# Two steps of a hybrid SSD and pooling trunk's first layer moved to later places in each engine's queue

## The chip, the cores and the metric

The kernel runs on one core of a Trainium2 chip. A core has five engines with a queue each: TensorE (PE, matrix products), VectorE (DVE), ScalarE (ACT), GpSimd (POOL) and SyncE (SP, which here only issues DMAs). An engine works through its queue in order, and an instruction at the head that waits for another engine holds up all behind it. The metric is the device time of one execution in microseconds; lower is better.

## The reference, cut to what matters

The kernel computes one inference step of two layers for 1024 prompt tokens and 64 sample tokens (8 sequences of 8), 1088 columns in all, with 1024 model channels:

```
hn   = rmsnorm(x, g) * (1 + scale) + shift        # scale, shift from the conditioning
z, xbc, dt = split(hn @ w_in)                     # first layer, 2048 + 4096 + 32 columns
xbc  = silu(causal_conv4(xbc))                    # 4 taps along the tokens
y    = ssd_scan(xbc, softplus(dt))                # chunked state space recurrence
x    = x + (1 + gate) * (norm(y * silu(z)) @ w_out)
hn   = ...; pooling layer with u, z = hn @ w_in   # second layer
y    = rmsnorm(x + ...)
```

All of it is float32. A product of two float32 numbers is made on TensorE from three products of parts: each operand is split into `hi`, its leading part, and `lo`, the difference.

## The kernel before, in words

Channels lie on the 128 partitions and tokens along the free dimension, so `x` is eight tiles of 128x1088, the channel tiles k = 0 to 7. The change touches the first layer's front only, the first 360 us or so of the program.

**Scaling.** `front` (L1308) goes over the eight channel tiles. For each, an `ada` product on TensorE gives the scale and shift (L253, L262; DVE reads them in L271 and L272), and `modulate` (L311) makes the scaled tile (DVE L316), its `hi` part (`hh`, ACT L322), its `lo` part (`hl`, DVE L323, which needs `hh`), the tile itself with its shift (ACT L324) and the same for the sample columns (L329 to L333). TensorE then multiplies tile k with two weight tiles (L182 to L184: `hi` by `hi`, `lo` by `hi`, `hi` by `lo`, in three column chunks each) and with the dt weights (`pdt`, L1354). After the eighth tile two more weight tiles follow in the same form, whose evictions to `z` are `gate_chunk`s on ACT (L869).

**Activation differences.** The other columns of the first layer are multiplied by a scheme with seven half-size products for two weight tiles at once (`fast_pair`, L992) in place of eight. It needs differences of blocks of the activations: `act_sums_front` (L1375) makes sixteen half tiles by DVE subtractions (`sub`, L1382, in place on `x`) and splits the results into `hi` (ACT L1385) and `lo` (DVE L1386): four tiles each for the products T2, T3 and T4, and for T1 into the upper half of `hn`. Its steps are traced behind the six `gate_chunk`s of the two weight tiles after the scaling, under `issue_after(the gate chunk)`, and in the first pair.

**Pairs.** `front_pairs` (L1416) makes twelve pairs in the order of the list FRONT: z2, z3, z4, b5, x5, z5, b7, x7, z6, b0, x0, z7. Each pair is the seven products B11, B21, T2, T3, T1, T4, B22, of 24 matmuls of 272 columns each (L987 to L989; L989 is the one that needs the weight's `lo`). The weights of a pair are sums and differences of four blocks made on POOL (L952 to L959, `sw` and `wr`), each split by `split_half` (L168): `hi` on ACT (L174) and `lo` on DVE, the fourth and sixth of a pair on POOL (L176). Every product call first has the split of three products later traced. So the POOL splits of a pair serve T3 and T4, and the one traced in B21 serves T1. Products are added up by DVE from PSUM (`put` and `add`, L998), and B11 is copied by ACT (L1013).

**Convolution.** A b or x pair ends with `proj_end` for both its tiles: `conv_tile` (L336) makes the first tap on ACT (L351), three taps on DVE for the 1024 prompt columns and the 64 sample columns (L349), and the silu on ACT (L352); the result goes to DRAM (L1448). In the kernel before, this is traced behind B22 of the same pair.

**dt.** `dt_phase` (L438) turns `pdt` into step sizes in a chain of small DVE and ACT operations (L443 to L506), with exponentials on ACT (L452, L479, L483) between silu evaluations, and copies on POOL (L436).

**What sets the order.** The instructions are written in plain order; when the program is built, a scheduler lays them into each engine's queue by the order in which they were traced and its own estimate of when they can start. `issue_after(i)` adds one constraint: instructions that the block traces on the engine of `i` stand behind `i`. A `gate_chunk` is an ACT instruction, so in the kernel before it holds back the ACT part of the activation differences and not their DVE part.

Of the kernel before, what the change touches and what calls it, by code (L numbers as in the profile page):

```python
# [2 lines left out]

# [4 lines left out]
F32 = mybir.dt.float32  # L8
F32R = mybir.dt.float32r
AF = mybir.ActivationFunctionType  # L10
ALU = mybir.AluOpType
# [86 lines left out]
class Build:  # L98
# [212 lines left out]
    def modulate(self, l, k, x, rst, hi, lo, a, n, t):  # L311

        nc = self.nc
        pn = min(a + n, NP) - a
        sh = self.shf[l][:, k, 8:9]
        nc.vector.scalar_tensor_tensor(out=t[:, :pn], in0=x[:, a:a + pn], scalar=self.scl[l][:, k, 8:9], in1=rst[:, a:a + pn], op0=ALU.mult, op1=ALU.mult)  # L316
        if l:
            nc.scalar.activation(t[:, :pn], t[:, :pn], AF.Identity, bias=sh)
            nc.scalar.activation(hi[:, a:a + pn], t[:, :pn], AF.Copy)
            nc.vector.tensor_tensor(out=lo[:, a:a + pn], in0=t[:, :pn], in1=hi[:, a:a + pn].bitcast(F32), op=ALU.subtract)  # L320
        else:
            nc.scalar.activation(hi[:, a:a + pn], t[:, :pn], AF.Identity, bias=sh)  # L322
            nc.vector.scalar_tensor_tensor(out=lo[:, a:a + pn], in0=t[:, :pn], scalar=sh, in1=hi[:, a:a + pn].bitcast(F32), op0=ALU.add, op1=ALU.subtract)  # L323
            nc.scalar.activation(t[:, :pn], t[:, :pn], AF.Identity, bias=sh)  # L324
        if pn < n:
            s = slice(NP, TOK)
            ts = t[:, pn:n].rearrange("p (b i) -> p b i", i=8)
            eng = nc.gpsimd if l and k % 2 == 0 else nc.vector
            eng.tensor_tensor(out=t[:, pn:n], in0=x[:, s], in1=rst[:, s], op=ALU.mult)  # L329
            eng.tensor_tensor(out=ts, in0=ts, in1=self.scl[l][:, k, 0:8].unsqueeze(2).to_broadcast([P, 8, 8]), op=ALU.mult)  # L330
            eng.tensor_tensor(out=ts, in0=ts, in1=self.shf[l][:, k, 0:8].unsqueeze(2).to_broadcast([P, 8, 8]), op=ALU.add)
            nc.scalar.activation(hi[:, s], t[:, pn:n], AF.Copy)
            eng.tensor_tensor(out=lo[:, s], in0=t[:, pn:n], in1=hi[:, s].bitcast(F32), op=ALU.subtract)  # L333


    def conv_tile(self, ti, raw, dst, ncv, scan):  # L336
# [172 lines left out]
    def scan_group(self, g, T):  # L509
# [167 lines left out]

        load_ac(0)
        F = [front(0)]
        yield  # L680
        F.append(front(1))
        yield
        for c in range(0, 8, 2):
# [624 lines left out]
    def front(self):  # L1308

        nc, io, sl = self.nc, self.io, self.slots  # L1310
        xs = self.xs
        wdts = sl.get("wdt")
        wdt = wdts[:, :256].rearrange("p (k m) -> p k m", k=8)
        nc.sync.dma_start(wdt, io["wdt"])
        rst = sl.get("rst")
        with self.ln_set():
            nc.scalar.activation(rst, xs[0], AF.Square)
            for k in range(1, 8):
                sq = self.raw_tile()
                for a, n in CH if k == 7 else ((0, TOK),):  # L1320
                    nc.scalar.activation(sq[:, a:a + n], xs[k][:, a:a + n], AF.Square)
                    nc.vector.tensor_tensor(out=rst[:, a:a + n], in0=rst[:, a:a + n], in1=sq[:, a:a + n], op=ALU.add)
            for a, n in CH:
                self.ms_log(rst, rst, a, n, 1.0 / 1024, "mm", 3)
                self.rstd(rst[:, a:a + n])
        self.ada_first(0)
        self.hn = []

        self.wslots = []
        for i in range(2):  # L1330
            self.stream_split(i, True)
        self.ada_first(1)
        ws = [self.wsplit.pop(i) for i in range(2)]
        self.wpos = 2
        pst = [[self.mm_tile() for _ in range(3)],
               [self.pp.tile([P, 512], F32, tag=t, bufs=b, name=self.name("p0")) for t, b in (("y", 2), ("y", 2), ("S", 1))]]
        pdt = self.pp.tile([P, 512], F32, tag="tr", bufs=2, name="pdt")
        for k in range(8):
            if k < 6:
                self.ada_first(k + 2)  # L1340
            if k == 4:
                self.stream_split(2)
            if k == 6:
                self.stream_split(3)
            hi, lo = sl.get("hh", F32R), sl.get("hl", F32R)
            for a, n in CH if k == 0 else ((0, TOK),):
                self.modulate(0, k, xs[k], rst, hi, lo, a, n, xs[k][:, a:a + n])
            self.hn.append((hi, lo))
            for i in range(2):
                for c in range(3):  # L1350
                    self.mm1(pst[i][c], ws[i], k, (hi, lo), CH[c], k == 0, k == 7)
            for j in range(4):
                n = 320 if j == 3 else 256
                nc.tensor.matmul(pdt[32 * j:32 * j + 32, :n], wdt[:, k, :], xs[k][:, 256 * j:256 * j + n],  # L1354
                                 start=k == 0, stop=k == 7, tile_position=(0, 32 * j))
        sl.free(rst, wdts, *self.wslots)
        dt = self.dt_phase(pdt)
        next(dt)
        for i in range(2):
            dst = sl.get("z")  # L1360
            for c in range(3):
                self.gate_chunk(dst, c, pst[i][c])
            self.gate_store(i, dst)
        ops = self.act_sums_front()
        for i in range(2):
            w, dst = self.stream_next(), sl.get("z")
            for c, ch in enumerate(CH):
                ps = self.mm_tile()
                self.mm3(ps, w, self.hn, ch)
                with self.tc.issue_after(self.gate_chunk(dst, c, ps).ins):  # L1370
                    next(ops)
            self.gate_store(2 + i, dst)
        self.front_pairs(ops, dt)
# [42 lines left out]
    def front_pairs(self, ops, dt):  # L1416

        nc, sl = self.nc, self.slots
        self.fast_init(len(FRONT))
        self.G, G = {}, None  # L1420
        for n, (kind, g) in enumerate(FRONT):
            if kind == "z":
                ts = [sl.get("z") for _ in range(2)]
                outs = [(t, 0, None) for t in ts]
            else:
                if kind == "b":
                    self.G[g] = G = self.proj_open(g)
                ii = 2 * (kind == "x")
                ts = [self.proj_begin(G, ii + i) for i in range(2)]
                outs = [(t, 3, t[:, 1027:1115].rearrange("p (b w) -> p b w", w=11)[:, :, 3:11]) for t in ts]  # L1430

            def after(x):
                if kind == "z" and x in ("z01", "z11"):
                    a = HALF * int(x[1])
                    self.z_chunk(ts[1], ts[1][:, a:a + HALF], a, HALF)
                elif kind == "z" and x in ("B21", "B22"):
                    a = HALF * (x == "B22")
                    self.z_chunk(ts[0], ts[0][:, a:a + HALF], a, HALF)
                    if x == "B22":
                        self.gate_store(2 * g, ts[0])  # L1440
                elif kind == "z" and x == "T4":
                    self.gate_store(2 * g + 1, ts[1])
                if kind != "z" and x == "B22":
                    for i in range(2):
                        self.proj_end(G, ii + i, ts[i])
                        if g:
                            t = G["out"].pop()
                            nc.sync.dma_start(self.xbd[g][ii + i], t)  # L1448
                            sl.free(t)
                if n == 0 and x in ("B11", "B21"):  # L1450
                    next(ops)
                if n < 2 and x in ("B21", "T3", "T4"):
                    next(dt, None)
                if n == len(FRONT) - 1:
                    if x in ("T2", "T3"):
                        sl.free(*[self.T[int(x[1]), k] for k in range(4)])
                    elif x == "T1":
                        for k in range(4):
                            for i in range(2):
                                nc.sync.dma_start(self.hn[k][i][:, HALF:].bitcast(F32), self.b12d[2 * k + i])  # L1460

            self.fast_pair(*outs, after)
        sl.free(*[self.T[4, k] for k in range(4)])

    def ssd_layer(self):
# [351 lines left out]
```

## Time and profile before

| what | value |
|---|---|
| median of 3 runs | 1618.24 us (1616.37 to 1619.92) |
| profiled execution: time | 1620.23 us |
| profiled execution: span, first to last instruction | 1618.5 us |
| TensorE busy over the span | 1581.7 us (98%) |
| DVE, ACT, POOL busy | 1288.2, 796.5, 500.8 us |
| mean granted TensorE clock | 0.993 |

A row of the timeline gives the start and the length of an instruction (or of several alike, x2), its engine, source line, operation, output and inputs, and in brackets how long the engine had been idle before it and what ended that. A row of the waits names the waiting engine and tile and who was waited for, then the sum, the count and the longest, in us. A row of windows gives a stretch, its length, the busy time of TensorE, of its weight loads, of DVE, ACT and POOL, then the granted TensorE clock, the DMA share and GB/s. The busy time of TensorE is not its time at peak, since its matmuls overlap; its idle times are what can be won.

### The profile page before, as it was taken

The numbers are of one execution on the slowest core, as the hardware profiler recorded it, in microseconds if no ns is written. First come the engines' busy times: TensorE is split into PE (matmuls) and PEld (weight loads), VectorE is DVE, ScalarE is ACT, GpSimd is POOL, SyncE is SP. The second block draws the span as 40 slices with busy tenths as digits, with TensorE's granted clock in tenths as the row PEclk, the third lists the DMA queues.
The fourth block names the chain that finished last, engine by engine and source line by source line (L and its number), as shares of the span: only waits on it lengthen the run. The fifth ranks groups of instructions, "written<-read, shape, count | busy, mean of one in ns | idle before, by whom it ended". The sixth has DMA issues, their size and how long they took to land. (4 is left out here: it accounts for less than half of the span.)

```text
span 1618.5 us, 30648 instructions
## 1 busy us (share of the span) xinstructions
PE 1581.7 (98%) x11916; PEld 1506.4 (93%) x11916; DVE 1288.2 (80%) x2148; ACT 796.5 (49%) x1517; POOL 500.8 (31%) x562
## 2 busy tenths in 40 slices
PE   8999999999999999999999999999999999999997
PEld 6799999998889889888898899999999999999997
DVE  5875779778888888788888867988889867577886
ACT  6653344357676766674555436623223233333364
POOL 0133556421221212120212222365666640000241
PEclk8999999999999999999999999999999999999999
DMA  9422232354555454668898632133333379555683
GB/s 344 169 85 91 94 117 69 110 186 139 201 161 175 157 192 148 234 210 300 293 338 279 216 128 93 45 139 115 106 106 103 115 223 364 164 165 180 160 176 120
DMA packets 122305, 275.58 MB, mean 170 GB/s; under 512 B 18192, under 2 KB 59312, under 8 KB 122160
## 3 DMA queue, kind: packets, MB, share of 16 engines
q1 hardware_dynamic: 118128, 260.90, 46.6%
q0 software_dynamic: 4032, 12.72, 4.5%
q8 instruction: 94, 1.54, 0.4%
q14 instruction: 51, 0.42, 0.1%
HBM read 201.12 MB, written 70.23 MB: 168 GB/s over the span
## 5 line engine op out<-in xcount | busy, mean ns | idle before, releaser
L989 PE MATMUL st<-hh,w 128*128 128x272 f32 x832 | 240.7, 289 | 2.1 <-DVE w L176 2.1
L987 PE MATMUL st<-hh,w 128*128 128x272 f32 x832 | 240.1, 289 | 0.0
L988 PE MATMUL st<-hl,w 128*128 128x272 f32 x832 | 239.9, 288 | 0.0
L987 PE MATMUL st<-t,w 128*128 128x272 f32 x624 | 179.7, 288 | 0.0
L989 PE MATMUL st<-t,w 128*128 128x272 f32 x624 | 179.5, 288 | 0.0
L182 PE MATMUL mm<-hh,wh 128*128 128x368 f32 (+1 forms) x528 | 178.7, 338 | 0.7 <-ACT raw L421 0.7
L988 PE MATMUL st<-t,w 128*128 128x272 f32 x624 | 179.2, 287 | 0.0
L183 PE MATMUL mm<-hl,wh 128*128 128x368 f32 (+1 forms) x528 | 173.6, 329 | 0.0
L184 PE MATMUL mm<-hh,wl 128*128 128x368 f32 (+1 forms) x528 | 173.4, 328 | 0.0
L989 PEld LDWEIGHTS st<-hh,w 128*128 128x128 f32 x832 | 156.4, 188 | 3.2 <-DVE w L176 3.2
L174 ACT ACTIVATE w<-wr 128x512 fp32r<-128x512 f32 x104 | 65.7, 631 | 188.8 <-PE st L989 155.5
L988 PEld LDWEIGHTS st<-hl,w 128*128 128x128 f32 x832 | 156.7, 188 | 0.0
L987 PEld LDWEIGHTS st<-hh,w 128*128 128x128 f32 x832 | 156.7, 188 | 0.0
L183 PE MATMUL mm<-gl,wh 128*128 128x368 f32 (+1 forms) x384 | 127.3, 331 | 3.6 <-DVE gl L750 3.5
L182 PE MATMUL mm<-gh,wh 128*128 128x368 f32 (+1 forms) x384 | 130.1, 340 | 0.6 <-ACT raw L419 0.5
L1204 PE MATMUL op<-b,w 128*128 128x272 f32 x448 | 128.9, 288 | 0.7 <-DVE b L1133 0.7
L1203 PE MATMUL op<-b,w 128*128 128x272 f32 x448 | 129.5, 289 | 0.0
L1205 PE MATMUL op<-b,w 128*128 128x272 f32 x448 | 128.9, 288 | 0.0
L184 PE MATMUL mm<-gh,wl 128*128 128x368 f32 (+1 forms) x384 | 127.0, 331 | 0.0
L604 POOL TENSOR_TENSOR hd<-h,cd 128x256 f32<-128x256 f32 x56 | 46.8, 836 | 233.2 <-DVE h L605 118.3
L987 PEld LDWEIGHTS st<-t,w 128*128 128x128 f32 x624 | 117.7, 189 | 0.1
L989 PEld LDWEIGHTS st<-t,w 128*128 128x128 f32 x624 | 117.3, 188 | 0.0
(298 smaller groups left out, 4544.6 us busy)
## 6 DMA issues: line engine op xcount, KB each, us to landing
wr<-win SPq DMA_DIRECT2D x48, 512.0 KB, 4.3
acb<-acd SPq DMA_DIRECT2D x64, 256.0 KB, 4.0
wr<-pin SPq DMA_DIRECT2D x32, 512.0 KB, 3.6
wr<-pout SPq DMA_DIRECT2D x28, 512.0 KB, 3.7
x<-x1d SPq DMA_DIRECT2D x24, 544.0 KB, 6.1
x1d<-x SPq DMA_DIRECT2D x22, 544.0 KB, 3.9
wr<-pout POOLq DMA_DIRECT2D x20, 512.0 KB, 5.7
x<-xT SPq DMA_DIRECT2D x16, 544.0 KB, 6.9
```

The source lines that it names most:

```text
L174: self.nc.scalar.activation(hi, src, AF.Copy)
L182: nc.tensor.matmul(ps[:, :n], hi[:, k, :], ah[:, a:a + n], start=first, stop=False)
L183: nc.tensor.matmul(ps[:, :n], hi[:, k, :], al[:, a:a + n], start=False, stop=False)
L184: nc.tensor.matmul(ps[:, :n], lo[:, k, :], ah[:, a:a + n], start=False, stop=last)
L604: nc.gpsimd.tensor_tensor(out=hd, in0=h[-1], in1=cd.unsqueeze(2).to_broadcast([P, 4, 64]), op=ALU.mult)
L987: nc.tensor.matmul(ps[c][:, :QUART], hi[:, k], xh[:, t], start=(k == 0), stop=False)
L988: nc.tensor.matmul(ps[c][:, :QUART], hi[:, k], xl[:, t], start=False, stop=False)
L989: nc.tensor.matmul(ps[c][:, :QUART], lo[:, k], xh[:, t], start=False, stop=(k == 3))
L1203: nc.tensor.matmul(ps[:, :QUART], hi[:, k], xh, start=k == 0, stop=False)
L1204: nc.tensor.matmul(ps[:, :QUART], hi[:, k], xl, start=False, stop=False)
L1205: nc.tensor.matmul(ps[:, :QUART], lo[:, k], xh, start=False, stop=k == 7)
```

## The change

Two places in the tracing order change; no arithmetic, shape, buffer or engine does.

1. `modulate` returns its last DVE instruction, and the activation differences traced behind the gate chunks stand under a second `issue_after`, that of the eighth channel tile's last DVE instruction. So the DVE subtractions may not stand ahead of it in the DVE queue.
2. The two `proj_end`s of a b or x pair, with the store to DRAM, are kept back as a closure and traced when the next pair has traced its second product, B21.

```
-            nc.vector.tensor_tensor(out=lo[:, a:a + pn], in0=t[:, :pn], in1=hi[:, a:a + pn].bitcast(F32), op=ALU.subtract)
+            last = nc.vector.tensor_tensor(out=lo[:, a:a + pn], in0=t[:, :pn], in1=hi[:, a:a + pn].bitcast(F32), op=ALU.subtract)
...
-            eng.tensor_tensor(out=lo[:, s], in0=t[:, pn:n], in1=hi[:, s].bitcast(F32), op=ALU.subtract)
+            last = eng.tensor_tensor(out=lo[:, s], in0=t[:, pn:n], in1=hi[:, s].bitcast(F32), op=ALU.subtract)
+        return last
...
-                self.modulate(0, k, xs[k], rst, hi, lo, a, n, xs[k][:, a:a + n])
+                last = self.modulate(0, k, xs[k], rst, hi, lo, a, n, xs[k][:, a:a + n])
...
-                with self.tc.issue_after(self.gate_chunk(dst, c, ps).ins):
+                with self.tc.issue_after(self.gate_chunk(dst, c, ps).ins), self.tc.issue_after(last.ins):
                     next(ops)
...
-        self.G, G = {}, None
+        self.G, G, ends = {}, None, []
+
+        def end(G, g, ii, ts):
+            for i in range(2):
+                self.proj_end(G, ii + i, ts[i])
+                if g:
+                    t = G["out"].pop()
+                    nc.sync.dma_start(self.xbd[g][ii + i], t)
+                    sl.free(t)
+
...
+                if x == "B21":
+                    while ends:
+                        ends.pop(0)()
                 if kind != "z" and x == "B22":
-                    for i in range(2):
-                        self.proj_end(G, ii + i, ts[i])
-                        if g:
-                            t = G["out"].pop()
-                            nc.sync.dma_start(self.xbd[g][ii + i], t)
-                            sl.free(t)
+                    ends.append(functools.partial(end, G, g, ii, ts))
...
+        for f in ends:
+            f()
```

What this does to the queues is shown at three places. Source lines of the changed file are higher by 1 up to `modulate` and by 2 behind it (L323 is L324 there, L1382 is L1384).

The DVE queue at channel tiles 5 to 7 before; `x_177`, `x_179`, `x_185`, `x_187`, `x_189` are the tiles 0, 1, 4, 5, 6, `hl_707` is the `lo` part of tile 6 and `am_652` the scale and shift of tile 7:

```order
L331 TENSOR_TENSOR x_187<-x_187,shf_267 128x64
L316 SCALAR_TENSOR_TENSOR x_189<-x_189,scl_269,rst_277 128x1024
L330 TENSOR_TENSOR x_189<-x_189,scl_269 128x64
L333 TENSOR_TENSOR hl_668<-x_187,hh_667 128x64
L331 TENSOR_TENSOR x_189<-x_189,shf_267 128x64
L1382 TENSOR_TENSOR x_185<-x_185,x_177 128x544
L1382 TENSOR_TENSOR x_179<-x_187,x_179 128x544
L271 TENSOR_SCALAR shf_267<-am_652,vec 128x9
L272 TENSOR_SCALAR scl_269<-am_652,adab_265,vec 128x9
L140 TENSOR_TENSOR wl_703<-wr_700,wh_702 128x1024
L323 SCALAR_TENSOR_TENSOR hl_707<-x_189,shf_267,hh_706 128x1024
```

Tile 6's `lo` part comes last here, behind two subtractions and tile 7's scale and shift. The DVE queue at the same place in the changed kernel:

```order
L334 TENSOR_TENSOR hl_668<-x_187,hh_667 128x64
L317 SCALAR_TENSOR_TENSOR x_189<-x_189,scl_269,rst_277 128x1024
L331 TENSOR_TENSOR x_189<-x_189,scl_269 128x64
L332 TENSOR_TENSOR x_189<-x_189,shf_267 128x64
L141 TENSOR_TENSOR wl_703<-wr_700,wh_702 128x1024
L324 SCALAR_TENSOR_TENSOR hl_707<-x_189,shf_267,hh_706 128x1024
L272 TENSOR_SCALAR shf_267<-am_652,vec 128x9
L273 TENSOR_SCALAR scl_269<-am_652,adab_265,vec 128x9
```

The two subtractions are gone from between tile 6's scaling and its `lo` part, and that part now stands ahead of tile 7's scale and shift. All sixteen subtractions stand behind the last instruction of tile 7.

The DVE queue at the end of a convolution (that of pair b5), before; `xbc_2054` and `xbc_2067` are the two results, `w_2120` the `lo` part of the weight for T1 of the next pair, x5, and `raw_2080<-st_2123` and `raw_2080<-st_2124` the two sums of that pair's B21:

```order
L349 SCALAR_TENSOR_TENSOR xbc_2054<-raw_1817,vec,xbc_2054 128x1024
L349 SCALAR_TENSOR_TENSOR xbc_2054<-raw_1817,vec,xbc_2054 128x64
L349 SCALAR_TENSOR_TENSOR xbc_2067<-raw_1820,vec,xbc_2067 128x1024
L176 TENSOR_TENSOR w_2120<-sw_1954,w_2120 128x512
L998 TENSOR_TENSOR raw_2080<-st_2123,u_2086 128x272
L998 TENSOR_TENSOR raw_2080<-st_2124,u_2086 128x272
```

Here the split and the sums come behind the whole convolution. The same in the changed kernel, where tiles traced behind the moved step have other numbers (`xbc_2125`, `xbc_2138`; `w_2094`; `raw_2054`):

```order
L177 TENSOR_TENSOR w_2094<-sw_1954,w_2094 128x512
L1000 TENSOR_TENSOR raw_2054<-st_2097,u_2060 128x272
L351 SCALAR_TENSOR_TENSOR xbc_2125<-raw_1817,vec,xbc_2125 128x64
L351 SCALAR_TENSOR_TENSOR xbc_2125<-raw_1817,vec,xbc_2125 128x1024
L1000 TENSOR_TENSOR raw_2054<-st_2098,u_2060 128x272
L351 SCALAR_TENSOR_TENSOR xbc_2125<-raw_1817,vec,xbc_2125 128x64
L351 SCALAR_TENSOR_TENSOR xbc_2138<-raw_1820,vec,xbc_2138 128x1024
```

The split for T1 now stands ahead of the last four instructions of the convolution, and the two sums stand between them. The same happens at all six b and x pairs; from the next sum on the queue is as before.

The POOL queue in the first pair, z2, before; `w_1012` is the split for T3, `w_1109` the one for T4, and the copy from `raw_772` belongs to the dt phase and waits for DVE L480:

```order
L436 COPY raw_1437<-raw_772 128x128
L176 TENSOR_TENSOR w_1012<-wr_892,w_1012 128x512
L959 TENSOR_TENSOR sw_996<-wr_786,sw_996 128x512
L952 TENSOR_TENSOR sw_1185<-wr_1140 128x512
L953 TENSOR_TENSOR sw_1185<-sw_1185,wr_894 128x512
L176 TENSOR_TENSOR w_1109<-wr_892,w_1109 128x512
L957 TENSOR_TENSOR wr_1140<-wr_894,wr_1140 128x512
```

Here the copy is first and the split for T4 next to last. The POOL queue at that place in the changed kernel:

```order
L177 TENSOR_TENSOR w_1012<-wr_892,w_1012 128x512
L961 TENSOR_TENSOR sw_996<-wr_786,sw_996 128x512
L954 TENSOR_TENSOR sw_1185<-wr_1140 128x512
L438 COPY raw_1437<-raw_772 128x128
L955 TENSOR_TENSOR sw_1185<-sw_1185,wr_894 128x512
L959 TENSOR_TENSOR wr_1140<-wr_894,wr_1140 128x512
L177 TENSOR_TENSOR w_1109<-wr_892,w_1109 128x512
```

The copy now stands between two sums of the next pair's weights, and the split for T4 one place later, behind L959 (L957 before).

Smaller moves: ACT makes four `hi` parts for T1 in a row before the last of T3, and the second and third exponential of the dt phase (L479, L483) stand some 12 ACT instructions later and apart, with one more pair of table loads. In the later pairs the POOL split for T4 stands ahead of the next pair's `raw` preparation (L376, L377), and SP issues the load of `scv` ahead of two stores (L1448) and not behind them. Behind pair z7 every queue is in the old order.

More of the change, by code (lines that the diff above doesn't have):

```diff
@@ L1 @@
 import contextlib
+import functools
 import itertools
@@ L319, in modulate @@
             nc.scalar.activation(hi[:, a:a + pn], t[:, :pn], AF.Copy)
[L320 removed]
+            last = nc.vector.tensor_tensor(out=lo[:, a:a + pn], in0=t[:, :pn], in1=hi[:, a:a + pn].bitcast(F32), op=ALU.subtract)
         else:
             nc.scalar.activation(hi[:, a:a + pn], t[:, :pn], AF.Identity, bias=sh)
[L323 removed]
+            last = nc.vector.scalar_tensor_tensor(out=lo[:, a:a + pn], in0=t[:, :pn], scalar=sh, in1=hi[:, a:a + pn].bitcast(F32), op0=ALU.add, op1=ALU.subtract)
             nc.scalar.activation(t[:, :pn], t[:, :pn], AF.Identity, bias=sh)
```

## The prediction

> **What bounds the kernel now.** I read the page first, then the waits of TensorE in the part that the change touches, then its timeline at these waits, then the engine it waits for. From the page:
>
> ```profile
> PE 1581.7 (98%) x11916; PEld 1506.4 (93%) x11916; DVE 1288.2 (80%) x2148; ACT 796.5 (49%) x1517; POOL 500.8 (31%) x562
> ```
>
> TensorE is idle for 36.8 us of the span of 1618.5, and it is the bound. The change removes no matmul, so it can win only idle time of TensorE, and only in the first 360 us, behind which all queues are as before. The waits of TensorE from 0 to 360 us (sum, count, longest):
>
> ```profile
> PE mm L182 <- ACT hh L322: 2.3, 2, 1.9
> PE st L989 <- DVE w L176: 2.1, 5, 0.4
> PE mm L183 <- DVE hl L323: 2.1, 2, 1.8
> ```
>
> The first row is the start of the scaling, ahead of any activation difference, and stays. The second is a weight's `lo` part that comes late, five times 0.42 us. The third holds one wait of 1.8 us for a tile's `lo` part. So 1.8 + 2.1 = 3.9 us is the most that the change can take from the waits, 0.24% of the time.
>
> **The activation differences.** TensorE, ACT and DVE around the 1.8 us (timeline):
>
> ```profile
> 63.60 0.76 PE L182 MATMUL mm<-hh,w 128*128 128x368 f32 x3
> 64.20 0.49 PE L182 MATMUL p<-hh,w 128*128 128x368 f32 x2
> 66.47 0.43 PE L183 MATMUL mm<-hl,w 128*128 128x368 f32 x1 [1.77 <-DVE hl L323]
> ```
>
> ```profile
> 59.96 1.14 ACT L322 ACTIVATE hh<-x,shf 128x1024 fp32r<-128x1024 f32 x1
> ```
>
> ```profile
> 60.21 3.54 DVE L1382 TENSOR_TENSOR x<-x,x 128x544 f32<-128x544 f32 x2
> 63.67 0.21 DVE L271 TENSOR_SCALAR shf<-am,vec 128x9 f32<-128x9 f32 x1
> 64.00 1.21 DVE L140 TENSOR_TENSOR wl<-wr,wh 128x1024 fp32r<-128x1024 f32 x1
> 65.14 1.27 DVE L323 SCALAR_TENSOR_TENSOR hl<-x,shf,hh 128x1024 fp32r<-128x1024 f32 x1
> ```
>
> `hh` of tile 6 is there at 61.10, but DVE first makes two subtractions for 3.54 us, then tile 7's scale and a weight split, and `hl` comes at 66.41. Without the two, `hl` starts at 65.14 - 3.54 = 61.6 and ends near 62.9; the new queue also puts it ahead of tile 7's scale. TensorE asks for it 0.3 us into the tile, at 63.9: about 1 us to spare. Tile 7 follows with the same work and no subtraction in it. So 1.77 us of waiting goes. Nothing takes its place here, as far as the waits show: of the four in the `hh` and `hl` rows this is the only one behind the first two tiles.
>
> The two subtractions were so slow because POOL worked beside them; POOL, and DVE later, with POOL idle:
>
> ```profile
> 60.15 1.29 POOL L953 TENSOR_TENSOR sw<-sw,wr 128x512 f32<-128x512 f32 x1
> 61.40 1.77 POOL L957 TENSOR_TENSOR wr<-wr,wr 128x512 f32<-128x512 f32 x1
> ```
>
> ```profile
> 71.17 1.35 DVE L1382 TENSOR_TENSOR x<-x 128x544 f32<-128x544 f32 x2
> ```
>
> Two cost 1.35 us alone and 3.54 us beside POOL. This stretch is now met by `hl` of tile 6 and the scaling of tile 7. If they are slowed by the same 2.2 us, `hl` ends near 65.1 in place of 62.9, 1.2 us late, and the gain is 0.6. I take 1.77, since the POOL rows end at 63.2 and the scale of tile 7 stands behind `hl`.
>
> The Trainium skill, "GPSIMD Engine Reference", section "8. Key points", says that GpSimd shares its SBUF interfaces with VectorE and contends with DVE instructions that have two SBUF inputs. The rows agree (1.35 against 3.54 us). By that rule `hl` (L323, two SBUF inputs) pays in full and the sum below would be 1.2 us smaller.
>
> **What the moved differences delay.** All sixteen now start when tile 7's last DVE instruction ends, near 66 us, and take 16 x 0.64 = 10 us (0.64 is the step of the row at 71.17), to some 77 us; before, half of them were made between the tiles, and the last row of them stands only a few behind the one at 71.17. The dt chain and the `lo` splits on DVE follow up to 1.5 us later, while TensorE arrives 1.77 us earlier. So their slack shrinks by about 3 us. The points where it can bite are the weight splits of pair z2. TensorE, ACT, DVE and POOL there:
>
> ```profile
> 97.32 0.29 PE L987 MATMUL st<-hh,w 128*128 128x272 f32 x1
> ```
>
> ```profile
> 112.36 0.28 PE L987 MATMUL st<-t,w 128*128 128x272 f32 x1
> ```
>
> ```profile
> 92.99 1.28 ACT L869 ACT_TABLE_LOAD   x1
> 94.29 0.48 ACT L869 ACTIVATE z<-mm 128x368 f32<-128x368 f32 x1
> ...
> 97.52 0.46 ACT L869 ACTIVATE z<-mm 128x352 f32<-128x352 f32 x1 [0.57 <-PE mm L184]
> ...
> 99.50 0.62 ACT L174 ACTIVATE w<-wr 128x512 fp32r<-128x512 f32 x1
> ```
>
> ```profile
> 99.84 0.68 DVE L176 TENSOR_TENSOR w<-sw,w 128x512 fp32r<-128x512 f32 x1
> ```
>
> ```profile
> 100.20 1.48 POOL L176 TENSOR_TENSOR w<-wr,w 128x512 fp32r<-128x512 f32 x1 [6.49 <-ACT w L174]
> 101.65 1.78 POOL L959 TENSOR_TENSOR sw<-wr,sw 128x512 f32<-128x512 f32 x1
> 107.00 1.35 POOL L952 TENSOR_TENSOR sw<-wr 128x512 f32<-128x512 f32 x1 [3.58 <-DMA wr<-win]
> 108.43 1.66 POOL L953 TENSOR_TENSOR sw<-sw,wr 128x512 f32<-128x512 f32 x1
> 110.05 1.74 POOL L176 TENSOR_TENSOR w<-wr,w 128x512 fp32r<-128x512 f32 x1
> 111.75 1.74 POOL L957 TENSOR_TENSOR wr<-wr,wr 128x512 f32<-128x512 f32 x1
> ```
>
> ```profile
> 117.05 1.28 POOL L959 TENSOR_TENSOR sw<-wr,sw 128x512 f32<-128x512 f32 x1 [3.56 <-DVE w L176]
> ```
>
> B11 starts at 97.32 and T4, the sixth product, at 112.36: 3.0 us each, 0.125 per matmul. T2, the third, needs its `lo` with its third matmul, at 103.6; the DVE row ended at 100.5. That is 3.1 us of slack, of which about 3 goes: a wait of 0 to 0.8 us.
>
> T4 needs its POOL split at 112.36 + 0.25 = 112.61, and it was done at 111.79: 0.8 us of slack. In the new queue TensorE is there at 110.84. The POOL chain hangs on the ACT split at 99.50. ACT's evictions follow TensorE: the one at 94.29 had waited for a table load that is now elsewhere, and starts near 92; four `hi` parts and one more stand ahead of the last eviction where two did, 3 x 0.6 us more (the length of such a part by the row at 99.50), so the split comes near 98.2, 1.3 us earlier, not 1.77. POOL then needs, from the row at 100.20 on: the split for T3, L959, 3.6 us for the DMA, L952, now the copy (128x128; a quarter of the 1.28 of a 128x512 row is 0.3, an estimate), L953, L957 and only then the split for T4. With the lengths of these rows that ends at 111.79 - 1.3 + 0.3 + 1.7 = 112.5, 1.6 us late. With 1.28 us each, which the row at 117.05 shows for POOL undisturbed, the six save up to 2 us and TensorE waits for nothing. A wait at T2 is paid once, since it moves T4's need too. DVE has idle time from 104 us in the new queue, since it waits for the sums of T2 and T3, so I stand nearer to the undisturbed end: a loss of 0.5 us, bounds 0 and 1.6.
>
> The two further table loads on ACT, 2 x 1.28 us, fall between 102 and 112 us; the next splits there are needed 5 us later, so they cost nothing unless ACT is that late.
>
> **The convolutions.** DVE at the end of pair b5's convolution, the `hi` part on ACT, and TensorE in T1 of the next pair:
>
> ```profile
> 184.25 10.80 DVE L349 SCALAR_TENSOR_TENSOR xbc<-raw,vec,xbc 128x1024 f32<-128x1024 f32 x8
> 194.97 0.69 DVE L176 TENSOR_TENSOR w<-sw,w 128x512 fp32r<-128x512 f32 x1
> 195.59 0.77 DVE L998 TENSOR_TENSOR raw<-st,u 128x272 f32<-128x272 f32 x2
> ```
>
> ```profile
> 186.35 0.62 ACT L174 ACTIVATE w<-sw 128x512 fp32r<-128x512 f32 x1
> ```
>
> ```profile
> 195.72 0.40 PE L989 MATMUL st<-hh,w 128*128 128x272 f32 x1 [0.42 <-DVE w L176]
> ```
>
> The `hi` part is ready at 187.0, and the `lo` part stands behind the convolution until 194.97. In the new queue four of the eight instructions, with two of the 1024 columns, stand behind it: at 1.3 us (10.80 / 8) each it comes 2.6 to 5 us earlier, against 0.42 needed. The wait goes at all five places: 5 x 0.42 = 2.1 us. What is queued behind the split does not change in sum: from the next sum on the queue is as before, so DVE gets there as late as now. The two sums that now stand inside the convolution could stall it, if B21 were not yet done: T1, at 194.9, follows T2 and T3, so B21 ended 6 us before, at 188.9, and DVE reaches the first sum near 191. The reserve is 2 us. POOL's split for T4 moves ahead of the `raw` preparation and comes earlier. SP's stores move by one or two us behind the silu, with no weight load close behind them. I take the whole 2.1; bounds 1.2 (if two places keep their wait) and 2.1.
>
> **The sum.** -1.8 + 0.5 - 2.1 = -3.4 us. Bounds: -3.9, and with every loss at its end -1.8 + 1.2 + 1.6 - 1.2 = -0.2. The profiled execution took 1620.2 us (span 1618.5 and 1.7 around it) and would take 1616.8; the median of the three runs, 1618.24, is 2.0 below it, and becomes 1614.8. A difference within 0.2% (3.2 us) is about what a measurement of this kernel cannot tell from no change, so the forecast lies just beyond that line.
>
> **What shifts it from run to run.** Windows of 3.4 us of TensorE:
>
> ```profile
> 728.20:731.60 3.40, 1.31 (x12) 0.62 (x4) 0.78 (x1) 2.20 (x3) 0.00 (x0) 1.00 0.96 320
> 731.60:735.00 3.40, 2.84 (x11) 2.84 (x12) 3.40 (x4) 0.00 (x0) 0.00 (x0) 0.50 0.59 201
> ```
>
> After a window in which TensorE was busy for 1.31 of 3.40 us, the next ran at half the clock (0.50); one such costs 1.7 us. The three runs spread over 3.5 us, twice that. Whether a wait falls into one window or is cut by its border can change with any shift, so a median of few runs moves by one such window either way. The Trainium skill, "TensorE: Matmul & The Clock Gate", section "What's actually happening", says that this window is free-running and does not start with the kernel. The rows agree with a length of 3.4 us, and no single run can show the rest; by that rule the change neither wins nor loses one on average, and the sum stays -3.4.
>
> **The rivals.**
> - The front gives its gain back: `hl` is still late beside POOL, or T4 waits the full 1.6 us. For it: the POOL rows of 1.7 us. Against it: DVE's idle time there. -3.9 + 1.7 = -2.2: 1616.0, within 0.2%.
> - The convolutions keep their wait, because DVE stands at the sums inside them until B21 is done and the split for T4 or B22 is late in its place. Against it: 2 us of reserve. -1.3: 1616.9.
> - Clock windows: two more at half clock than before, +3.4 us: 1618.2, no change.
> - Slower: POOL stands at the copy that waits for the dt phase's L480, which hangs on ACT's L479, now some 12 instructions later. I put L480 near 104 and POOL there near 107. Each us that L480 comes after 107 is a us of TensorE at T4; from 110.4 the gain is gone, from 113.7 the kernel is slower by over 0.2%. At 115 it is +4.6: 1622.8. Against it: ACT has only four splits, a table load and three `t` between.
>
> **How the numbers follow.** The forecast has 0.57 and its own range is 1613.0 to 1615.0 (the bound of 3.9 us and one clock window more, to the 0.2% line). The front's giving back has 0.17, the convolutions 0.05, the clock windows 0.10 (0.02 of it beyond the line to slower), the copy 0.11. So faster by over 0.2%: 0.57; within: 0.17 + 0.05 + 0.08 = 0.30; slower: 0.11 + 0.02 = 0.13. The predicted time is 1614.8. The range, 1612.6 to 1618.2, takes in the first three cases and most of the fourth.
>
> **What would show it.** In the profile after, the row of PE for `hl` of the first layer holds one wait of 0.3 us and not two; the row of L989 for DVE's weight is gone; no wait of TensorE for a POOL weight at T4 above 0.5 us; `hl` of tile 6 ends before 64. DVE's last subtraction ends near 77. Wrong would make it: a wait of L989 for POOL near 111 us of 1.5 us or more, DVE idle inside a convolution ahead of a sum, or POOL idle ahead of the copy.

## The result, and the profile after

The changed kernel took 1614.61 us (median of 22 runs) against 1617.66 us of the kernel before beside it: 0.9984 of its time, 95% interval 0.9978 to 0.9991. The medians differ by 3.05 us, and the ratio stands for 2.6. The forecast was 1614.8. Two later comparisons gave 0.9993 (0.9981 to 1.0006) and 0.9988 (0.9978 to 0.9998). The mean of the three ratios is 0.9988, which is 1.9 us less. So the direction and the range of the prediction held. Its terms, shown below, did not all hold.

From the page of the changed kernel:

```profile
PE 1577.4 (98%) x11916; PEld 1505.4 (93%) x11916; DVE 1292.5 (80%) x2148; ACT 796.6 (49%) x1519; POOL 500.3 (31%) x562
```

Its span is 1612.5 us, 6.0 below the first trace of before. Only a part of this is the change, since the idle time of TensorE went down by 1.7 us (36.8 to 35.1) and its busy time by 4.3: the trace of before has five windows of 3.4 us at half clock up to 1600 us, that of after three. The waits of TensorE from 30 to 362 us of the changed kernel (sum, count, longest):

```profile
PE st L991 <- POOL w L177: 1.7, 1, 1.7
PE st L989 <- ACT w L175: 0.9, 2, 0.5
PE mm L183 <- ACT hh L323: 0.5, 1, 0.5
PE st L991 <- DVE w L177: 0.4, 2, 0.2
```

The wait for `hl` and the five waits for DVE's `lo` part are gone, as forecast. In their place stand a wait of 1.7 us for POOL and, at two places, one of 0.5 us for ACT with one of 0.2 us for DVE right behind it.

**A yardstick.** Take one matmul of the scaling (the first of channel tile 3) and one matmul ahead of the scan's start, the same two in every trace. Between them lies all that the change does to the waits of TensorE. TensorE's timeline before, and after:

```profile
48.22 0.43 PE L182 MATMUL mm<-hh,w 128*128 128x368 f32 x1
...
361.81 0.33 PE L182 MATMUL mm<-hh,wh 128*128 128x368 f32 x1
```

```profile
46.16 0.43 PE L183 MATMUL mm<-hh,w 128*128 128x368 f32 x1
...
357.61 0.33 PE L183 MATMUL mm<-hh,wh 128*128 128x368 f32 x1
```

The stretch took 361.81 - 48.22 = 313.59 us before and 357.61 - 46.16 = 311.45 us after: 2.14 us less. The same difference is worked out for every kernel below. It repeats to 0.1 us (before: 313.59 and 313.67; after: 311.45 and 311.44), except where a window at half clock falls into it: one more trace of the changed kernel, with one such window, took 313.02. The times of whole runs of one kernel spread over 5 us and more.

### The profile page after: what moved, and what is told of

The parts are those of the page before. It is cut to its first block, busy times and chain, and to the rows that moved or that the text cites. A ratio compares the mean times of both kernels' runs of the same rounds, so it can differ in the third digit from the quotient of the medians.

```text
span 1612.5 us, 30639 instructions
## 1 busy us (share of the span) xinstructions
PE 1577.4 (98%) x11916; PEld 1505.4 (93%) x11916; DVE 1292.5 (80%) x2148; ACT 796.6 (49%) x1519; POOL 500.3 (31%) x562
```

## The experiments

**The kernel before, the changed kernel, and each part alone.** The edits of the latter two, against the changed kernel:

```
# first part only
-                if x == "B21":
-                    while ends:
-                        ends.pop(0)()
...
-                    ends.append(functools.partial(end, G, g, ii, ts))
+                    end(G, g, ii, ts)
# second part only
-                with self.tc.issue_after(self.gate_chunk(dst, c, ps).ins), self.tc.issue_after(last.ins):
+                with self.tc.issue_after(self.gate_chunk(dst, c, ps).ins):
```

> The kernel before, once more, without an edit: what two sets of runs of one kernel differ by, and a second trace. Every theory: within 1.5 us of the other runs of the kernel before. The trace tells whether the waits behind 360 us (L750 2.65 us, L1103 1.72 us, L574 1.58 us) and the windows at half clock stand at the same places in every execution. If the waits ahead of 360 us (1.77 us for the lo part of tile 6, five of 0.42 us) are there again, they belong to the kernel; the windows at half clock ahead of 60 us (three in the first trace of before, one in that of after) should differ if their place is chance.

> The changed kernel, once more: its second trace. Theory A (waits): TensorE waits again 1.73 us at T4 of the first pair and at two B22s, so that the idle time ahead of 360 us is about as long as before, and the time differs from before by no more than 1.5 us in the mean. Theory B (the gain is real and lies in something else, for instance in fewer windows at half clock): 3 us faster again, with fewer windows at half clock than in the second trace of before.

> Only the first part: the differences stand behind the last scaling, and the convolutions are where they were. From the traces of before and after, with what follows a wait counted in: the wait for the lo part goes (-2.1 us) and the one at T4 of the first pair comes (+2.0 us), so -0.1 us: no change. The prediction had -1.8 + 0.5 = -1.3 us. If this part alone gives 2 to 3 us, the gain is in the windows at half clock or later in the program.

> Only the second part: the convolutions are traced behind B21 of the next pair, and the differences stay where they were. The prediction had -2.1 us. From the traces of before and after, with what follows a wait counted in: five waits of 0.7 us go and two new ones of 1.1 us at B22 come, -1.2 us, of which the start of the scan (a wait for the load of acb) gives some back: -0.2 to -1.2 us.

All four stood on one chip. The kernel before against itself gave 0.9998 (0.9985 to 1.0012), the changed one 0.9993 (0.9981 to 1.0006), the first part alone 0.9992 (0.9979 to 1.0006), the second alone 1.0001 (0.9989 to 1.0013). With such intervals (some 2 us either way) none of them can be told from no change by its time, and the traces must decide. In the second trace of before the waits ahead of 360 us are the same (five of 0.4 us, one of 1.8), but L1103's wait behind them, 1.7 us in the first trace, is 0.5 us there, and two windows at half clock stand ahead of 60 us in place of three: these come and go in one and the same program. In the second trace of the changed kernel the waits of the first are there again, at the same places, as the first of the two theories said. In the order of the four runs above, the stretch took 313.67, 313.02, 314.15 and 312.55 us. The waits up to 362 us of the first part alone, and of the second alone:

```profile
PE st L991 <- DVE w L177: 2.2, 5, 0.4
PE st L991 <- POOL w L177: 1.7, 1, 1.7
PE mm L183 <- ACT hh L323: 0.5, 1, 0.5
```

```profile
PE mm L184 <- DVE hl L324: 1.8, 1, 1.8
PE st L989 <- ACT w L175: 0.9, 2, 0.5
PE mm L183 <- ACT hh L323: 0.5, 1, 0.5
PE st L991 <- DVE w L177: 0.4, 2, 0.2
```

So the wait for POOL comes with the first part and the waits for ACT with the second, as the traces of before and after had said. The second trace of the changed kernel is 1.57 us longer than the first with the same waits. Windows in it (stretch, length, busy time of TensorE, its weight loads, DVE, ACT, POOL, granted clock, DMA share, GB/s):

```profile
108.00:111.40 3.40, 1.65 (x14) 1.44 (x13) 2.50 (x4) 2.58 (x3) 1.95 (x2) 1.00 0.13 12
111.40:114.80 3.40, 3.40 (x18) 3.40 (x17) 0.89 (x2) 0.46 (x1) 0.00 (x0) 0.50 0.36 142
```

TensorE stood still for 1.75 us of the window up to 111.4, at the wait for POOL, and ran the next at half clock. 313.02 - 311.45 = 1.57 us is what that costs. The trace of the first part alone has such a window at the same place. Taken out, the first part alone is 1.1 us shorter than before (314.15 - 1.57 - 313.67), the second also 1.1 (312.55 - 313.67), and both 2.2: the parts add up. For the first part the expectation of -0.1 had too small a gain; what it missed is shown with the prediction's first term below.

**The wait at T4.** TensorE and POOL of the changed kernel there:

```profile
109.41 0.40 PE L991 MATMUL st<-t,w 128*128 128x272 f32 x1 [1.73 <-POOL w L177]
```

```profile
95.64 2.32 POOL L177 TENSOR_TENSOR w<-wr,w 128x512 fp32r<-128x512 f32 x1 [5.24 <-ACT w L175]
97.92 1.74 POOL L961 TENSOR_TENSOR sw<-wr,sw 128x512 f32<-128x512 f32 x1
103.25 1.72 POOL L954 TENSOR_TENSOR sw<-wr 128x512 f32<-128x512 f32 x1 [3.58 <-DMA wr<-win]
104.91 0.29 POOL L438 COPY raw<-raw 128x128 f32<-128x128 f32 x1
105.16 1.28 POOL L955 TENSOR_TENSOR sw<-sw,wr 128x512 f32<-128x512 f32 x1
106.41 1.73 POOL L959 TENSOR_TENSOR wr<-wr,wr 128x512 f32<-128x512 f32 x1
108.10 1.26 POOL L177 TENSOR_TENSOR w<-wr,w 128x512 fp32r<-128x512 f32 x1
```

The split for T4 (the last row) ends at 109.36. Ahead of it stands L959, a difference for the next pair's weights, 1.73 us. In the kernel before it stood behind the split. The first edit below puts only this back. The second edit, made later, makes the split twice and so adds one POOL instruction in front of TensorE.

```
# split for T4 first          (sp: the split's own instruction; in split_half)
+        if n == 5:
+            self.t4 = sp
...
+            with self.tc.issue_after(self.t4.ins) if m == 1 else contextlib.nullcontext():
                 nc.gpsimd.tensor_tensor(out=z[:, f], in0=u[:, f], in1=z[:, f], op=ALU.subtract)
# split for T4 twice
+        for _ in range(2 if n == 5 and not self.later else 1):
             eng.tensor_tensor(out=lo, in0=src, in1=hi.bitcast(F32), op=ALU.subtract)
```

> The changed kernel, with one POOL instruction moved: the subtraction of the next pair's weights (L957 before, L959 after) stands behind the split for T4 of the first pair, as it did in the kernel before, and not ahead of it. Theory A (the front's gain is given back by the order on POOL): the 1.73 us wait at T4 goes, 2.0 us with what follows it, and with it the window at half clock at 111 us that two of three traces with this wait show (1.6 us each): 2 to 3 us faster than the changed kernel, 3 to 4 us faster than before. Rival (POOL is late in any order, because its rows are 1.7 us long beside DVE): a wait of 0.5 us or more stays there, and less than 1 us is won.

With the split first the time was 0.9979 (0.9967 to 0.9992), 3.4 us less than before, and the stretch 310.24 us, 1.2 less than the changed kernel's. That is less than the 2 to 3 us expected. The wait went from 1.73 us to 0.5 and not to nothing, though L959 took 1.73, since the split itself now took 0.5 us longer. In the kernel with both mends below, whose POOL order is the same:

```profile
106.79 1.73 POOL L177 TENSOR_TENSOR w<-wr,w 128x512 fp32r<-128x512 f32 x1
```

So both sides were partly right: 1.2 us of the wait was the order, and the rest was the length of POOL's rows.

> The changed kernel, with the split for T4 of the first pair made twice on POOL (same result): one more POOL instruction of 1.3 to 1.7 us ahead of TensorE there, and nothing else. Theory A (T4 hangs on POOL's chain, us for us): the wait at T4 grows from 1.73 to 3.0 to 3.4 us, the kernel is 1.3 to 1.7 us slower than the changed one, and a window at half clock, which came in two of four traces with a wait of 1.73 us, comes behind it in nearly every execution, another 0.8 us in the mean: about 1 us slower than before. Rival (POOL's order is not what holds T4): the wait stays as it is and the time does not change.

```profile
PE st L993 <- POOL w L178: 3.4, 1, 3.4
```

```profile
110.80:114.20 3.40, 0.78 (x6) 0.78 (x7) 1.45 (x1) 1.67 (x2) 2.49 (x2) 0.99 0.00 0
114.20:117.60 3.40, 3.40 (x17) 3.40 (x17) 0.44 (x1) 0.00 (x0) 0.00 (x0) 0.50 0.39 154
```

One POOL instruction of 1.59 us more made the wait 1.66 us longer (3.39 against 1.73), and a window at half clock followed. The stretch grew by 314.61 - 311.44 = 3.17 us, which is the instruction's 1.6 and the 1.57 of one window. The time became 1.0010 (0.9998 to 1.0021) of before, against 0.9988 (0.9978 to 0.9998) of the changed kernel on the same chip. Its expectation:

> The changed kernel a third time, beside the two below on the same chip. By the waits that its traces and those of before show, ahead of 360 us: -2.1 + 2.0 (first part) and -3.5 + 2.3 (second part), so 1.3 us faster than before, and 1 to 3 us faster as measured so far.

That run is the changed kernel's third, the one compared with here; its stretch was 311.44 us. T4 hangs on POOL's chain, us for us, in the one trace of each.

**The waits at B22.** ACT in pair z5, with the convolution of x5 inside it, in the kernel before and then in the changed one, and TensorE of the changed one:

```profile
215.64 2.31 ACT L352 ACTIVATE xbc<-xbc 128x1088 f32<-128x1088 f32 x2 [4.13 <-DVE xbc L349]
218.15 0.66 ACT L869 ACTIVATE z<-z 128x544 f32<-128x544 f32 x1 [0.19 <-DVE z L998]
218.71 0.61 ACT L174 ACTIVATE w<-sw 128x512 fp32r<-128x512 f32 x1
```

```profile
216.25 0.66 ACT L871 ACTIVATE z<-z 128x544 f32<-128x544 f32 x1 [8.35 <-DVE z L1000]
216.81 2.10 ACT L354 ACTIVATE xbc<-xbc 128x1088 f32<-128x1088 f32 x2
218.82 0.61 ACT L175 ACTIVATE w<-sw 128x512 fp32r<-128x512 f32 x1
```

```profile
219.48 0.39 PE L989 MATMUL st<-hh,w 128*128 128x272 f32 x1 [0.48 <-ACT w L175]
219.71 0.29 PE L990 MATMUL st<-hl,w 128*128 128x272 f32 x1
220.21 0.39 PE L991 MATMUL st<-hh,w 128*128 128x272 f32 x1 [0.21 <-DVE w L177]
```

In the kernel before, ACT made the two silus of the convolution first, and the silu of `z` and the `hi` part of the weight for B22 right behind them. In the changed kernel the silu of `z` has come first. It stands for 8.35 us, since it hangs on a sum which DVE makes inside the convolution, and the two silus, 2.1 us, now lie between it and the `hi` part. TensorE waits for that in two of the three pairs in which a z pair follows a convolution, at 219 and 284 us; in z7 the order on ACT is the same, but TensorE does not wait. The edit holds the two silus behind that `hi` part. It leaves DVE's order as it was; near 351 us, in z7, one POOL instruction and two weight loads also change places:

```
-                if x == "B21":
+                if x == "T3":
...
-        self.nc.scalar.activation(hi, src, AF.Copy)
+        self.hs = self.nc.scalar.activation(hi, src, AF.Copy)
...
+            with self.tc.issue_after(self.hs.ins):
                 nc.scalar.activation(dst, dst, AF.Silu)
```

> The changed kernel, with the two silus of a moved convolution held behind the hi part for B22 on ACT; every other queue is the same. Theory A (the hi part stands behind silus that wait for a later DVE): the two waits at B22 go, 2 x 1.1 us with what follows, so 2.3 us faster than the changed kernel and 3.5 us faster than before. Rival (given back): the start of the scan at 360 us waits for the load of acb in any case, and the wait of y there grows by what is won: 1 us or less.

> Both: the changed kernel with the split for T4 ahead on POOL and the silus behind the hi part for B22. Theory A: no wait of TensorE between 36 us and 360 us above 0.2 us; 4.3 us faster than the changed kernel, 5.6 us faster than before, if nothing is given back, and 4 us if the start of the scan takes 1.5 us of it. Rival (chance): the windows at half clock and the loads later on hide it, within 2 us of before.

> Only the second part, with the silus behind the hi part for B22; the differences stay where they were in the kernel before, and so do the wait for the lo part of tile 6 and POOL's order. Theory A: five waits of 0.7 us with what follows go and none comes: 3.5 us faster than before, less 0.5 to 1 us at the start of the scan. Against the run with both mends it prices the first part with T4 in order: 2.1 us.

ACT of the first of these, which has T4's wait and the mended silus, at the same place:

```profile
216.04 0.66 ACT L872 ACTIVATE z<-z 128x544 f32<-128x544 f32 x1 [7.37 <-DVE z L1001]
216.60 0.61 ACT L175 ACTIVATE w<-sw 128x512 fp32r<-128x512 f32 x1
217.12 2.10 ACT L355 ACTIVATE xbc<-xbc 128x1088 f32<-128x1088 f32 x2
```

The `hi` part ends at 217.2 and not at 219.4, and both waits went. Counted matmul by matmul, this kernel gains on the changed one at two places alone, 1.2 us near 218 and 1.15 near 283, and nothing in z7. The waits up to 362 us of the kernel with both mends:

```profile
PE st L995 <- POOL w L177: 0.5, 1, 0.5
PE mm L185 <- ACT hh L325: 0.5, 1, 0.5
```

The times were 0.9971 (0.9960 to 0.9983), 0.9955 (0.9941 to 0.9968) and 0.9974 (0.9964 to 0.9984), so 4.7, 7.3 and 4.2 us less than before. The stretches were 309.08, 307.86 and 310.10 us. The version with both mends beats both kernels: its stretch is 5.8 us shorter than before and 3.6 shorter than the changed one. Its expectation missed one thing, the 0.5 us at T4.

> The kernel with both mends, and the next pair's second sum on POOL (L953 before) also behind the split for T4 of the first pair. With both mends a wait of 0.50 us was left at T4. Theory A: it goes, 0.5 to 0.8 us faster than with both mends, 7 to 8 us faster than before. Rival: the split waits for its hi part on ACT instead (ready at 105.6, where POOL would come to it), or the weights of the next pair come late and the wait moves there: no faster than with both mends.

```
+            with self.tc.issue_after(self.t4.ins) if m == 1 and not self.later else contextlib.nullcontext():
                 nc.gpsimd.tensor_tensor(out=s[:, l], in0=s[:, f], in1=u[:, f], op=ALU.subtract)
```

The split now starts at 106.11 and takes 1.28 us; of the waits between 30 and 362 us only the 0.5 us for `hh` stays, which all kernels have. The stretch is 307.08 us, the shortest, 0.8 below that with both mends. The time, 0.9964 (0.9951 to 0.9978), cannot tell it from that one, since the two intervals overlap. The expected gain over that one, 0.5 to 0.8 us, is shown by the trace and not by the time. Against before, 7 to 8 us were expected, and the stretch gives 6.6.

**All together.** The stretch against before (313.63, the mean of its two traces), with one window at half clock (1.57 us) taken out of those marked, and the change of the whole time by the ratio times 1618:

| kernel | stretch, us | against before | whole time | 95% interval |
|---|---|---|---|---|
| changed (three comparisons) | 311.45, 313.02*, 311.44 | -2.2 | -2.6, -1.1, -1.9 | -3.6 to +1.0 over all three |
| first part alone | 314.15* | -1.1 | -1.3 | -3.4 to +1.0 |
| second part alone | 312.55 | -1.1 | +0.2 | -1.8 to +2.1 |
| changed, T4's split first | 310.24 | -3.4 | -3.4 | -5.3 to -1.3 |
| changed, silus behind B22's `hi` | 309.08 | -4.6 | -4.7 | -6.5 to -2.8 |
| changed, both | 307.86 | -5.8 | -7.3 | -9.5 to -5.2 |
| second part alone, silus mended | 310.10 | -3.5 | -4.2 | -5.8 to -2.6 |
| changed, both, one POOL sum later | 307.08 | -6.6 | -5.8 | -7.9 to -3.6 |
| changed, T4's split twice | 314.61* | -0.6 (+1.0 with the window) | +1.6 | -0.3 to +3.4 |

Each interval of the whole time holds the value of the stretch (the last one that with the window). So the gain and loss ahead of 362 us are enough to explain what was measured; with intervals of 1 to 2 us either way, an effect behind it of about 1 us is not excluded.

The matmuls can also be followed one by one through two traces, since each has the same 11916. From the yardstick's start on, the changed kernel's lead over the kernel before (times of the latter) grows by 0.74 us between 50 and 53 us, by 2.1 at 66 and by 0.2 near 72; it falls by 2.0 at 112, grows by 0.7 at each of the five places of the old wait for DVE's `lo` part, and falls by 1.2 and 1.15 at the two B22s. There is no other step above 0.12 us. The first part alone shows the first four, and the window's 1.5; the second alone shows the rest.

## Why the prediction was right, and where it was not

The forecast of -3.4 us met -3.05, the difference of the medians, in the first comparison. But the stretch gives -2.2 for the changed kernel, and the mean of the three comparisons is -1.9; so the close match was partly chance. The first term was too small, the loss in the front too small as well, and the convolutions' term left out two new waits.

- **`hl` of tile 6 (-1.8).** The wait went. `hl` took 2.31 us beside POOL, and TensorE did not wait for it. DVE after (`hl` of tile 6, the scaling of tile 7, its `hl`, and the last subtraction):

```profile
56.07 2.31 DVE L324 SCALAR_TENSOR_TENSOR hl<-x,shf,hh 128x1024 fp32r<-128x1024 f32 x1
...
59.55 2.31 DVE L317 SCALAR_TENSOR_TENSOR x<-x,scl,rst 128x1024 f32<-128x1024 f32 x1
...
63.08 1.28 DVE L324 SCALAR_TENSOR_TENSOR hl<-x,shf,hh 128x1024 fp32r<-128x1024 f32 x1 [0.83 <-ACT hh L323]
...
74.57 0.73 DVE L1384 TENSOR_TENSOR x<-x 128x544 f32<-128x544 f32 x1
```

  The Trainium skill, "GPSIMD Engine Reference", section "8. Key points", has DVE contend with GpSimd where DVE reads two SBUF inputs. The two rows of L324 agree, 2.31 us beside POOL and 1.28 without. The prediction had a case in which `hl` of tile 6 and the scaling of tile 7 (L317) are 2.2 us slower together and TensorE waits for 1.2 us. The two were slower by 2.1 us (1.03 each), but `hl` ended at 58.38, and TensorE asks for it only at 61.01. The last subtraction ended at 75.3, in a trace whose yardstick starts 2.1 us earlier: the 77 of the forecast. The term was too small: in kernels without T4's wait the first part is worth 310.10 - 307.08 = 3.0 us, not 1.8. The wait of 1.77 us is worth 2.1 of it, and 0.75 was not foreseen at all: the first part also changes TensorE's own queue, which the list of changed queues ahead of the prediction leaves out. In the kernel before, the eight dt matmuls of tile 3 stand apart, with matmuls of the last column chunk between them. TensorE before, and after:

```profile
51.19 0.62 PE L1354 MATMUL pdt<-x,wdt 128*32 128x256 f32 x2
...
52.57 0.47 PE L1354 MATMUL pdt<-x,wdt 128*32 128x256 f32 x3
...
52.81 0.39 PE L1354 MATMUL pdt<-x,wdt 128*32 128x256 f32 x2
...
52.88 0.43 PE L1354 MATMUL pdt<-x,wdt 128*32 128x320 f32 x1
...
54.11 0.44 PE L182 MATMUL mm<-hh,w 128*128 128x368 f32 x1
```

```profile
49.76 0.75 PE L1356 MATMUL pdt<-x,wdt 128*32 128x256 f32 x8
...
51.30 0.44 PE L183 MATMUL mm<-hh,w 128*128 128x368 f32 x1
```

  The eight stand together after the change, in 0.75 us. Before, two of them alone take 0.62. From the yardstick's first matmul to the next tile's first it is 54.11 - 48.22 = 5.89 us before and 51.30 - 46.16 = 5.14 after, with the same work. The first part alone has the new order and 5.14 us, the second alone the old order and 5.88. No list of waits shows this, since TensorE is busy all the time. Why the scheduler laid them so was not looked into.

- **The loss in the front (+0.5).** This is the step that failed. The prediction put the wait at T4 between 0 and 1.6 us and took 0.5, since it said that DVE had idle time there and POOL was nearly undisturbed. The trace has the upper end, 1.73 us idle, and 2.0 us of time (309.08 - 307.08, with T4's wait and without). A wait for POOL of 1.5 us or more there was one of the signs of being wrong that the prediction named. Four of the six POOL rows from the split for T3 on (95.64 to 108.10, without the copy) stand at 1.7 us or above, as three of them did in the trace of before, so "nearer to the undisturbed end" was wrong; DVE's rows run on without a break from 105.21 to 109.91. That the wait came out at the forecast's upper end is luck. Counted from the yardstick's start, TensorE asked for the split 2.9 us earlier than before (at 61.5 us against 64.4) and not 1.77, and the split ended 0.4 us earlier (at 63.2 against 63.6) and not 0.7 later. The rival "the front gives its gain back" named this with 0.17. It was what happened in the front; its total of -2.2 equals the stretch's by chance, since it kept the whole 2.1 for the convolutions. The order on POOL, which the prediction had described word for word, was the main cause: with L959 behind the split, 0.5 us of the 1.73 is left. The wait also brought a window at half clock in two of five traces that have it at 1.73 to 1.75 us; that is another 0.6 us in the mean (2/5 x 1.57, an estimate from five traces), counted nowhere in the forecast of this step.
- **T2 (0 to 0.8).** No wait appeared there. Nor did the copy on POOL wait for the dt phase (the slower rival): it ran at 104.91, as soon as the sum ahead of it was done.
- **The convolutions (-2.1).** All five waits went, and DVE did not stand at a sum inside a convolution. With the silus mended the second part is worth 3.5 us, 0.7 for each wait of 0.42: 0.3 us more than the idle time that the trace shows. Against this came the two waits at B22, 0.65 us of idle time each, and (311.45 - 309.08) / 2 = 1.2 us of time each. The net is -1.1, and the failed sentence is "what is queued behind the split does not change in sum". It held for DVE. On ACT the silu of `z` had moved ahead of the convolution's two silus and waited there for DVE, and the `hi` part stood behind all three. That the net lies near this term's bound of 1.2 is chance: the bound stood for two places that keep their wait, and none did.
- **The clock.** As forecast, it moves single runs by more than the change. One window costs 1.57 us, near the 1.7 of the prediction, and the traces of all kernels show three to six of them up to 1600 us. In the statement of the forecast's own range, the 1613.0 does not fit its reason: 3.9 and 1.7 below 1618.2 is 1612.6, the end of the whole range.

The sum by the traces is then -3.0 + 2.0 - 3.5 + 2.4 = -2.1, and +0.6 for the window, -1.5.

Two things stay open. Behind 362 us the queues are the same, but the waits of the scan's start (L621 before, L623 after) added up to between 0.2 and 2.4 us in these traces, and to 0.2 and 1.2 in two traces of the kernel before alone; whether an earlier TensorE loses part of its gain there was not separated from this spread. And why POOL's undisturbed length (1.28 us) shows in some rows and 1.7 in others was seen beside DVE instructions, but not tried by itself.

## What to carry to other kernels

When a block of work is moved out of one engine's way, read the new order of every other engine up to the next product that needs it, TensorE's own queue too: both losses here came from an order (POOL's L959, ACT's silus) and 0.75 us of the gain from TensorE's. Where a chain of several instructions has one length beside a busy neighbour and another without, take the length that the neighbouring rows show. To judge a change of 0.1%, measure the time between two fixed instructions in the traces: it repeated to 0.1 us here, where the interval of a comparison of a dozen runs was some 2 us either way.

## What was not expected of the hardware

- A wait of 1.73 to 1.75 us at one place gave a window at half clock in two of five traces, one of 1.77 us at another place in none of four, one of 3.39 in the only one, one of 0.5 in none of two. With windows laid so that their borders fall on the changes of the granted clock, TensorE was busy for 1.66 of 3.41 us ahead of the two at half clock, and for 1.68 in two of the others; in the fifth a border cut the wait, and the window had 2.39. So a window that is about half busy can be enough. A sharp limit is not shown: in the trace with both mends one of 2.17 us was followed by half clock and one of 1.64 was not. The Trainium skill, "TensorE: Matmul & The Clock Gate", section "What's actually happening", has the throttle come back after an idle window; by these rows the window need not be idle throughout.
- A wait of TensorE cost some 0.3 us more than its idle time wherever it was measured: 0.42 us of idle time was worth 0.7, 0.50 us at T4 was worth 0.8, 1.73 us there 2.0, 1.77 us at tile 6 2.1, and the two stops at a B22, 0.65 us together, 1.2. The cause of the 0.3 was not looked into.
